# Eight quarter steps of the modulation rows m2 and m5, moved from the h2 stage into the rwkv stage

## The chip, the cores and the metric

The kernel runs on one core of a Trainium2 chip. The metric is the device time of one execution in microseconds (us). The core's engines are PE (TensorE, matmuls), DVE (VectorE), ACT (ScalarE), POOL (GpSimd) and SP (SyncE, which here mostly issues DMAs). Each engine executes its own list of instructions in order; engines wait for each other and for DMAs through semaphores.

## What is computed

Two transformer-like blocks run one after the other on 512 tokens of width 1024. The first is modulated by a conditioning vector (adaLN) and mixes an RG-LRU with dilated attention. The second makes a mixture of three branches (a multi-scale pooling, a differential attention, and a bidirectional rwkv-like recurrence) and ends in 32 experts. Each block's modulation is a long vector of silu(c) times a weight matrix:

```
mod = jnp.einsum('bd,de->be', jax.nn.silu(c), w_ada) + b_ada     # 1 row x (n*1024)
h   = rms_norm(x, g) * (1.0 + scale) + shift                     # shift, scale: rows of mod
x   = x + gate * ...                                             # gate: a row of mod
```

The second block has six such rows of 1024 numbers. Two of them, here m2 (the gate of the mixture's result) and m5 (the gate of the experts' result), are read for the first time near the end of the program: the mixture's residual and the experts' sum. The other four are needed for the norms.

## The kernel before

The program is one long function for one core. Its parts in order of time are: the first block; the h2 stage (the norm of its result x1, modulated and transposed into four pairs of tiles h2h and h2l, high and low parts of fp32); the rwkv stage; the differential attention; the merge of the branches (pm, wbr), the output projection (po) and the router; and the experts, in which the wires of the DMA queues carry 387 GB/s nearly without a break.

Nobody writes the order of instructions by hand. The code is written in one sequence, and a scheduler turns it into one list per engine: at each point it takes, of the instructions whose inputs are there, the one that was written first. So where a piece is written sets its rank, and where it lands follows from what is ready. Tiles come from pools with fixed numbers of buffers; the pool for weights has two raw buffers (512 KB each), three high parts and three low parts in this stretch, and they are handed out in the order in which the code is written. A later tile waits until the buffer it is given has been read for the last time.

**Modulation rows.** `row_steps` (L373) makes one row in four quarters of 256 columns. One quarter (L376 to L393) loads 256 numbers of bias on SP, loads two pieces of the weight matrix (512 KB each, L298), multiplies them by silu(c) in 16 matmuls (L384, m2p or m5p), copies the four partial sums out of PSUM on ACT (L386), adds them in one matmul (L388), adds the bias on DVE (L389; for m2 also a scale, L391) and stores 256 numbers to DRAM on SP (L392). The generators of all rows stand in the list `fill`, and `step(n)` (L352) runs the next n quarters of it wherever the code calls it. Of 28 quarters, 20 are run inside the dilated attention of the first block. The last eight (m2 and m5, four each) are run at two places of the h2 stage: four ahead of `norm_rows` (`step(MS[3])`, L1079) and four behind `mod_T` (`step(MX)`, L1084).

**The rwkv stage** (L1087 on) has twelve batches. `batch(n)` (L1336) writes, for batch n, `ph_a` (L1128: the products pA of receptance and key tiles, and their transposes ptb), `ph_i` (L1178: the pieces for the triangular inverse), and for the batch before it the DVE loop `ph_s` (62 operations on LT), and for batch n-2 `ph_b` (L1206: the inverse's last steps pi, px, pW, pz, and the recurrence in chunks, 16 pch matmuls and the DVE updates SI each). Written between them, but of lower rank, are projections of h2: `proj_tok` (tile pt, 256 columns; q, k and v) and `proj_feat` (tile pf, 512 columns; keys, pooling and gates). A projection needs one weight buffer, converted by ACT (wh, L305) and DVE (wl, L306), and three matmuls for each product (L311 to L313). They fill PE where a batch waits.

On PE the recurrence of one batch ends with two groups of pch matmuls, one for each chunk. The second group of a batch serves below as the mark of how far the recurrence is: in the trace that of batch 1 begins at 707.5 us, that of batch 4 at 828.4, that of batch 7 at 948.3, that of batch 8 at 979.2, and that of batch 11, the last, at 1084.8. The stretch from one such mark to the next is called a run.

Of the kernel before, what the change touches and what calls it, by code (L numbers as in the profile page):

```python
# [186 lines left out]
def build(tc, A, out, dbg=None, upto=99):  # L187
    with ExitStack() as ctx:
        _build(ctx, tc, A, out, dbg, upto)


def _build(ctx, tc, A, out, dbg, upto):
# [89 lines left out]
    def cc(name):  # L282
        g, o, w = _COFF[name]
        return csts[g][:, o:o + w]
# [67 lines left out]
    def step(n=1):  # L352

        while n and fill:
            try:
                next(fill[0])
                n -= 1
            except StopIteration:
                fill.pop(0)
# [276 lines left out]


    yb = []
    MX = 4
    MS, MA = (0, 0, 0, 4), (3, 2)  # L640
    bias1 = cc("bias1")
    def att_scores(ft, e):

# [273 lines left out]
    def cstep(n=1):  # L917
        for _ in range(n):
            next(cx, None)
# [163 lines left out]
    cstep(99)  # L1083
    step(MX)  # L1084

# [21 lines left out]
    def w1(name, shape=(4, 64), bufs=1, dt=F32):  # L1107
        p = rp if name == "AZ" else rpa if name in EARLY else rpb
        return p.tile([128] + list(shape), dt, tag=name, name=name, bufs=bufs)

    def bc(ap, sh):
        return ap.to_broadcast(sh)
# [65 lines left out]
    def ph_i(d, AMB, bi):  # L1178

        for e in range(2):  # L1180
            for i in range(2):
                r0 = 64 * e + 32 * i
                SY.dma_start(atD[bi][e, i].rearrange("q s t -> s q t"),
                             AMB[r0:r0 + 32, e, :, :, 32 * i:32 * i + 32].rearrange("p s f t -> p (s f) t"))
        LT = w1("LT", (32, 32), 2)
        for g in range(4):
            SY.dma_start(LT[32 * g:32 * g + 32].rearrange("p s t -> p (s t)"),
                         atD[bi].rearrange("e i q s t -> (e i q) (s t)"))
        return LT

    def ph_s(d, LT, bi):

        T = w1("Ti", (8, 32), 2)
        SY.dma_start(T.rearrange("p j t -> p (j t)"), A["tinit"])
        tmp = w1("Tm", (8, 32))
        for s in (range(31) if d == 0 else range(31, 0, -1)):
            js, ts_ = (slice(0, s // 4 + 1), slice(s + 1, 32)) if d == 0 else (slice(s // 4, 8), slice(0, s))
            nj, n = js.stop - js.start, ts_.stop - ts_.start
            V.tensor_tensor(tmp[:, :nj, :n], bc(LT[:, s, None, ts_], [128, nj, n]),  # L1199
                            bc(T[:, js, s:s + 1], [128, nj, n]), ALU.mult)  # L1200
            V.tensor_tensor(T[:, js, ts_], T[:, js, ts_], tmp[:, :nj, :n], ALU.add)  # L1201
        td = ttD[bi].rearrange("e i q (j g) t -> g (e i q) j t", g=4)
        for g in range(4):
            SY.dma_start(td[g], T[32 * g:32 * g + 32])
# [122 lines left out]
    def run_b():  # L1327
        n, sts = pend.pop(0)
        ph_b(*sts)
        if n == 3 and dbg is not None and "S_c" in dbg:  # L1330
            for d_ in range(2):
                for e, rows in par:
                    SY.dma_start(dbg["S_c"][128 * d_:128 * d_ + 128][rows, 256 * e:256 * e + 256],
                                 SI[d_, e][rows].rearrange("p a b -> p (a b)"))

    def batch(n):  # L1336
        d, chs = batches[n]
        AMB = w1("AMB", (2, 2, 4, 192), 3)
        sts = {c - min(chs): ph_a(d, c, c - min(chs), AMB) for c in chs}
        LT = ph_i(d, AMB, n % 4)  # L1340
        while loops:
            ph_s(*loops.pop(0))
        loops.append((d, LT, n % 4))
        pend.append((n, (d, chs, sts, AMB, n % 4)))
        if len(pend) > 2:
            run_b()
# [42 lines left out]
        GP.memset(t, 0.0)  # L1389
    for n in range(4, 12):  # L1390
        batch(n)
    ph_s(*loops.pop(0))
    while pend:
        run_b()
# [744 lines left out]
```

## Time and profile before

| | before |
|---|---|
| median of three runs | 1863.11 us (1859.43 to 1864.79) |
| the profiled execution | 1868.35 us |
| its span in the profile | 1866.5 us |
| PE busy | 1715.4 us (92% of the span) |
| DVE busy | 1068.7 us (57%) |
| ACT busy | 617.4 us (33%) |
| POOL busy | 230.4 us (12%) |

The profile is of one execution. The span runs from the first to the last instruction; the execution's own time is 1.9 us longer. An engine's busy time is the time in which it executes at least one instruction. PE has two clock levels, 1.2 and 2.4 GHz, and the profile gives the mean granted clock of a stretch as a share of the higher one: 1.00 is 2.4 GHz throughout.

### The profile page before, as it was taken

What the parts mean: (1) busy time and instruction counts of PE and PEld (TensorE: products, weight loads), DVE (VectorE), ACT (ScalarE), POOL (GpSimd) and SP (SyncE); (2) the same over time, 40 slices, a digit from 0 to 9 for tenths busy, and PEclk for the clock granted to TensorE, in tenths of its full rate; (3) what the DMA queues carried; (4) which work ended last, traced back from release to release, by engine and by line L of the source; (5) the groups of instructions that cost most, each with busy time, mean ns of one, the idle gap of its engine ahead of it and who ended that gap; (6) DMA issues with size and microseconds to landing.
All of it is one profiled execution on the core that took longest, in us unless ns stands there. A gap on an engine that the chain in (4) does not pass through costs nothing.

```text
span 1866.5 us, 31358 instructions
## 1 busy us (share of the span) xinstructions
PE 1715.4 (92%) x12309; PEld 1216.4 (65%) x12310; DVE 1068.7 (57%) x2489; ACT 617.4 (33%) x1154; POOL 230.4 (12%) x254
## 2 busy tenths in 40 slices
PE   5899998977998899999999969989799999999998
PEld 3884577964665777888888846779644544444444
DVE  3545577374578856989888538865513333432332
ACT  4324555453443232344333324542311111111010
POOL 0110003001104102212200015100100001010100
PEclk8999999987898998999999989999899999999999
DMA  8335723467847555556654367628189999999997
GB/s 295 126 110 198 237 79 124 160 213 210 232 130 183 158 171 126 157 166 157 181 142 122 102 225 240 223 67 311 46 302 387 386 386 386 387 387 387 386 386 275
DMA packets 277744, 417.34 MB, mean 224 GB/s; under 512 B 105788, under 2 KB 128856, under 8 KB 277336
## 3 DMA queue, kind: packets, MB, share of 16 engines
q1 hardware_dynamic: 248696, 384.88, 61.7%
q10 hardware_dynamic: 25568, 16.78, 2.9%
q0 software_dynamic: 3328, 13.63, 2.6%
q8 instruction: 98, 1.61, 0.4%
q14 instruction: 54, 0.44, 0.1%
HBM read 371.70 MB, written 43.53 MB: 222 GB/s over the span
## 4 chain that ended last, share of the span: by engine, by line
PE 73%; DVE 11%; DMA 7%; ACT 3%; issue 3%; SPq 2%; POOL 1%; ACTq 0%; DVEq 0%; POOLq 0%
PE ped L1983 7%; PE peg L1944 6%; PE peu L1951 6%; PE pf L311 5%; PE pf L313 4%; PE pf L312 4%; PE pcb L2015 3%; PE po L1806 2%; PE pt L311 2%; PE pt L313 2%; PE pt L312 2%; PE pg L1917 2%; PE pg L1918 2%; DVE Tm L1199 1%; DMA kb<-kbD 1%
## 5 line engine op out<-in xcount | busy, mean ns | idle before, releaser
L306 DVE TENSOR_TENSOR wl<-wr,wh 128x1024 fp32r<-128x1024 f32 x125 | 153.5, 1228 | 65.0 <-ACT wh L305 63.4
L305 ACT ACTIVATE wh<-wr 128x1024 fp32r<-128x1024 f32 x125 | 131.8, 1056 | 171.5 <-PE pf L312 91.9
L311 PE MATMUL pf<-h2h,wh 128*128 128x512 f32 x344 | 144.5, 420 | 10.7 <-ACT wh L305 4.7
L312 PE MATMUL pf<-h2l,wh 128*128 128x512 f32 x344 | 142.4, 414 | 0.0
L313 PE MATMUL pf<-h2h,wl 128*128 128x512 f32 x344 | 141.2, 410 | 0.0
L1983 PE MATMUL ped<-wd,hid 128*64 128x512 f32 (+1 forms) x528 | 127.6, 585 | 0.7 <-ACT hid L1967 0.7
L1944 PE MATMUL peg<-wg,hTg 128*64 128x512 f32 x512 | 127.0, 597 | 0.0
L1951 PE MATMUL peu<-wu,hTg 128*64 128x512 f32 x512 | 125.1, 594 | 0.0
L2016 DVE TENSOR_TENSOR acc<-acc,pcb 128x512 f32<-128x512 f32 (+1 forms) x124 | 75.9, 665 | 47.0 <-PE pcb L2015 46.8
L1989 POOL TENSOR_TENSOR yl<-ey,yh 128x512 fp32r<-128x512 f32 x30 | 38.3, 1278 | 468.1 <-ACT yh L1988 468.1
L1199 DVE TENSOR_TENSOR Tm<-LT,Ti 128x60 f32<-128x60 f32 (+24 forms) x372 | 86.3, 232 | 14.0 <-DMA LT<-atD 5.3
L1201 DVE TENSOR_TENSOR Ti<-Ti,Tm 128x60 f32<-128x60 f32 (+24 forms) x372 | 82.2, 221 | 8.6
L1951 PEld LDWEIGHTS peu<-wu,hTg 128*64 128x64 f32 x512 | 43.8, 137 | 65.2 <-issue 62.8
L311 PEld LDWEIGHTS pf<-h2h,wh 128*128 128x128 f32 x344 | 67.5, 196 | 28.8 <-ACT wh L305 5.2
L1983 PEld LDWEIGHTS ped<-wd,hid 128*64 128x64 f32 x528 | 39.4, 136 | 71.4 <-issue 67.7
L1944 PEld LDWEIGHTS peg<-wg,hTg 128*64 128x64 f32 x512 | 41.8, 137 | 60.9 <-issue 58.1
L313 PEld LDWEIGHTS pf<-h2h,wl 128*128 128x128 f32 x344 | 66.8, 194 | 21.9 <-issue 5.6
L312 PEld LDWEIGHTS pf<-h2l,wh 128*128 128x128 f32 x344 | 67.3, 196 | 17.7 <-issue 3.0
L1988 ACT ACTIVATE yh<-ey 128x512 fp32r<-128x512 f32 x30 | 18.9, 630 | 166.7 <-DVE ey L1987 94.4
L1921 ACT ACTIVATE hTg<-pg,sh,gs 128x128 f32<-128x128 f32 x64 | 28.2, 456 | 121.7 <-PE peu L1951 55.4
L1924 DVE TENSOR_SCALAR hTg<-pg,gs,sh 128x128 f32<-128x128 f32 x64 | 25.3, 409 | 75.3 <-PE peu L1951 38.4
L311 PE MATMUL pt<-wh,h1h 128*128 128x256 f32 x192 | 56.4, 296 | 6.7 <-ACT q L547 4.3
(958 smaller groups left out, 4309.4 us busy)
## 6 DMA issues: line engine op xcount, KB each, us to landing
wg<-in_w_exp_gate_dram SPq DMA_DIRECT2D x64, 1024.0 KB
wu<-in_w_exp_up_dram SPq DMA_DIRECT2D x64, 1024.0 KB
wd<-in_w_exp_down_dram SPq DMA_DIRECT2D x62, 1024.0 KB
wr<-in_w_in_dram SPq DMA_DIRECT2D x97, 512.0 KB
kb<-kbD SPq DMA_DIRECT2D x24, 384.0 KB
wr<-in_w_out_dram SPq DMA_DIRECT2D x16, 512.0 KB
LT<-atD SPq DMA_DIRECT2D x48, 128.0 KB
thD<-mth ACTq DMA_DIRECT2D x24, 256.0 KB
```

The lines of the kernel that those rows point to most:

```text
L305: SC.activation(hi, raw, AF.Copy)
L306: V.tensor_tensor(lo, raw, hi.bitcast(F32), ALU.subtract)
L311: PE.matmul(p, ah, bh, start=start, stop=False)
L312: PE.matmul(p, ah, bl, start=False, stop=False)
L313: PE.matmul(p, al, bh, start=False, stop=stop)
L1199: V.tensor_tensor(tmp[:, :nj, :n], bc(LT[:, s, None, ts_], [128, nj, n]), bc(T[:, js, s:s + 1], [128, nj, n]), ALU.mult)
L1201: V.tensor_tensor(T[:, js, ts_], T[:, js, ts_], tmp[:, :nj, :n], ALU.add)
L1944: mm = PE.matmul(pg[64 * a:64 * a + 64, :], hT[:, k, 64 * a:64 * a + 64], gp[a][k // 4][:, k % 4, :], start=(k == 0), stop=(k == 7), tile_ ...
L1951: PE.matmul(pu[64 * a:64 * a + 64, :], hT[:, k, 64 * a:64 * a + 64], up[a][k // 4][:, k % 4, :], start=(k == 0), stop=(k == 7), tile_posit ...
L1983: PE.matmul(pd[64 * a:64 * a + 64, :], hid[:, m * k + 64 * a:m * k + 64 * a + 64], dn[q][a][:, k, 0:q1 - q0], start=(k == 0), stop=(k == 3 ...
L2015: PE.matmul(p, ohT[R, 128 * i:128 * (i + 1)], yy[R, qs], start=(z == 0), stop=(z == len(parts) - 1))
L2016: V.tensor_tensor(acc[i][:, qs], acc[i][:, qs], p, ALU.add)
```

## The change

The two calls in the h2 stage run no quarters any more, and behind each of the batches 4 to 11 one quarter is written. What is computed stays the same.

```
@@ -636,8 +636,8 @@
     yb = []
-    MX = 4
-    MS, MA = (0, 0, 0, 4), (3, 2)
+    MX = 0
+    MS, MA = (0, 0, 0, 0), (3, 2)
@@ -1389,6 +1389,7 @@
     for n in range(4, 12):
         batch(n)
+        step(1)
     ph_s(*loops.pop(0))
```

What the scheduler makes of it stands at three places. Lines of the changed kernel behind L1391 have one line number more.

First, SP's list between the last stores of the first block and the first weights of the h2 projections. `m2b`, `m5b` are the bias and the result of a quarter, `m5w2r` a raw weight piece of its third quarter, `wr` a raw weight tile of the projections, `kbD` the stored keys of the recurrence, `cst` constants. Before:

```order
L379 DMA m5b<-in_bada_2r_dram 1x256
L298 DMA m5w2r<-in_w_ada_dram 128x1024
L392 DMA m2D<-m2b 1x256
L298 DMA m5w3r<-in_w_ada_dram 128x1024
L392 DMA m5D<-m5b 1x256
L379 DMA m5b<-in_bada_2r_dram 1x256
L298 DMA m5w3r<-in_w_ada_dram 128x1024
L392 DMA m5D<-m5b 1x256
L379 DMA m5b<-in_bada_2r_dram 1x256
L392 DMA m5D<-m5b 1x256
L275 DMA cst_4502<-in_cst_dram 128x514
L298 DMA wr<-in_w_in_dram 128x1024 x2
```

After:

```order
L778 DMA kbD_2113<-nb 512x1x64 x2
L275 DMA cst_4328<-in_cst_dram 128x514
L778 DMA kbD_2113<-nb 512x1x64
L778 DMA kbD_2113<-tha 512x1x64 x3
L778 DMA kbD_2113<-nb 512x1x64
L778 DMA kbD_2113<-tha 512x1x64
L298 DMA wr<-in_w_in_dram 128x1024 x5
L1132 DMA kb<-kbD_2113 128x768
L1134 DMA kr<-kkD 128x256
```

The sixteen weight pieces of the eight quarters (the last ones are shown) and all bias loads and stores are gone from here; five weight tiles of the projections follow the stores of the keys directly.

Second, PE in the rwkv stage, in the run of batch 2 (the one that begins at 707.5 us in the trace of before). `pA`, `ptb`, `pi`, `px`, `pta`, `pW` belong to a batch, `pgt` to the rwkv gate, `pt` to a projection. Before:

```order
L1260 MATMUL pi<-T_6772,AMB 32x32 x5
L879 MATMUL pgt<-gl,gw_6490 128x512
L1260 MATMUL pi<-T_6772,AMB 32x32 x11
L311 MATMUL pt<-wh,h2h_4315 128x256
L312 MATMUL pt<-wl,h2h_4315 128x256
L313 MATMUL pt<-wh,h2l_4316 128x256
L311 MATMUL pt<-wh,h2h_4326 128x256
L312 MATMUL pt<-wl,h2h_4326 128x256
L313 MATMUL pt<-wh,h2l_4327 128x256
L1162 MATMUL pA<-AR,BK 128x128 x8
L311 MATMUL pt<-wh,h2h_4337 128x256
L312 MATMUL pt<-wl,h2h_4337 128x256
```

After:

```order
L1255 MATMUL pi<-cst_75,TT_4341 32x32 x4
L384 MATMUL m2p<-m2w0r,st_945 32x256 x8
L1162 MATMUL pA<-AR,BK 128x128 x8
L1260 MATMUL pi<-T_6598,AMB 32x32 x16
L388 MATMUL m2q<-m2r,cst_75 1x256
L1171 MATMUL ptb<-cst_75,BK 128x64 x8
L1265 MATMUL pi<-TT_4341,T_6598 32x32 x16
L1273 MATMUL px<-AZ,TT_4341 64x128 x16
L1232 MATMUL pta<-cst_75,AR 64x64 x9
```

The eight quarters land in three runs, those of the batches 2, 3 and 4, and not one behind each of eight batches. The projections that stood in these runs (192 pt and 96 pf matmuls) are written later than the first quarters, take the same two raw buffers in that order, and move behind them: the runs hold batch work and quarters, and behind the last pch group there now stand 123 pf matmuls ahead of the first of the attention, where there were none.

Third, PE at the start of the differential attention. `dpl` are its scores, `dpt` and `dpo` the transposes and products of its probabilities, `pm` transposes the normalised recurrence output `gy`, which is loaded from DRAM (L1611) once the last chunk has been stored. Before:

```order
L1313 MATMUL pch<-WW,SI_4531 64x64
L1664 MATMUL dpl<-ks,qs 128x512 x2
L1617 MATMUL pm<-gy_11744,cst_75 128x512 x2
L1665 MATMUL dpl<-kl,qs 128x512
L1664 MATMUL dpl<-ks,qs 128x256
L1665 MATMUL dpl<-kl,qs 128x256
L1665 MATMUL dpl<-kl,qs 128x512
L1664 MATMUL dpl<-ks,qs 128x256
L1665 MATMUL dpl<-kl,qs 128x256
L311 MATMUL pf<-h2h_4315,wh 128x512
L312 MATMUL pf<-h2l_4316,wh 128x512
L313 MATMUL pf<-h2h_4315,wl 128x512
```

(The last three rows begin 48 pf matmuls of the gates.) After, around the first pm:

```order
L1665 MATMUL dpl<-ks,qs 128x512
L1666 MATMUL dpl<-kl,qs 128x512
L1665 MATMUL dpl<-ks,qs 128x256
L1666 MATMUL dpl<-kl,qs 128x256
L1691 MATMUL dpo<-v,aT 128x128 x4
L1691 MATMUL dpo<-vc,aT 128x128 x2
L1665 MATMUL dpl<-ks,qs 128x512
L1666 MATMUL dpl<-kl,qs 128x512
L1665 MATMUL dpl<-ks,qs 128x256
L1666 MATMUL dpl<-kl,qs 128x256
L1684 MATMUL dpt<-cst_75,P 128x128 x6
L1618 MATMUL pm<-gy_11744,cst_75 128x512
```

Before, two score matmuls stood between the last pch and the first pm. After, the 123 pf matmuls and the scores of the first three rounds, with the transposes and products of the earlier ones, stand ahead of the first pm, which come one at a time.

## Rows read from the trace of the kernel before

**Rows 1.** The page: the chain that ended last, share by engine

```profile
PE 73%; DVE 11%; DMA 7%; ACT 3%; issue 3%; SPq 2%; POOL 1%; ACTq 0%; DVEq 0%; POOLq 0%
```

**Rows 2.** Windows: from:to, length, busy PE, PEld, DVE, ACT, POOL; PE clock, DMA share, GB/s

```profile
433.00:469.00 36.00, 22.05 (x175) 8.76 (x175) 17.10 (x33) 12.80 (x27) 5.51 (x11) 0.78 0.82 258
469.00:707.50 238.50, 219.54 (x1426) 162.95 (x1426) 172.54 (x417) 94.24 (x149) 38.64 (x56) 0.92 0.62 169
707.50:828.40 120.90, 114.59 (x1277) 95.81 (x1276) 100.21 (x326) 44.90 (x91) 27.54 (x39) 0.95 0.57 145
828.40:1086.70 258.30, 247.37 (x2878) 212.24 (x2877) 201.53 (x628) 95.57 (x181) 32.94 (x52) 0.97 0.56 157
1086.70:1101.40 14.70, 1.20 (x5) 0.48 (x3) 0.85 (x2) 0.38 (x1) 1.32 (x2) 0.62 0.80 282
1200.00:1246.00 46.00, 35.61 (x216) 31.38 (x216) 31.66 (x56) 24.18 (x50) 5.59 (x5) 0.89 0.09 27
```

**Rows 3.** The chain of waits, h2 stage: start, length, what

```profile
453.53 5.10 DMA m5w2r<-in_w_ada_dram
...
463.12 4.63 DMA wr<-in_w_in_dram
467.78 1.06 ACT wh L305
```

**Rows 4.** Timeline of PE, h2 stage: start, length, what, [idle before]

```profile
444.67 0.64 PE L384 MATMUL m2p<-m2w2r,st 128*32 128x256 f32 x8 [1.33 <-DMA m2w2r<-in_w_ada_dram]
...
447.99 0.38 PE L388 MATMUL m2q<-m2r,cst 128*1 128x256 f32 x1
...
468.89 0.79 PE L311 MATMUL pf<-h2h,wh 128*128 128x512 f32 x1 [4.73 <-ACT wh L305]
...
479.31 0.40 PE L312 MATMUL pf<-h2l,wh 128*128 128x512 f32 x1
```

**Rows 5.** ACT by line from 440 to 469 us: busy, mean ns

```profile
L453 ACT ACTIVATE h2h<-h 128x512 fp32r<-128x512 f32 x8 | 4.9, 627 | 1.7 <-DMA vTD<-vTs 1.7
L449 ACT ACTIVATE h<-h2T,sh,gs 128x512 f32<-128x512 f32 x4 | 3.1, 774 | 0.3 <-PE h2T L436 0.3
```

**Rows 6.** Timeline of ACT, h2 stage: a row copy ahead of the first h

```profile
442.09 0.38 ACT L386 ACTIVATE m2r<-m2p 128x256 f32<-128x256 f32 x1 [2.86 <-PE m2p L384]
```

**Rows 7.** Windows: the run of batch 8, and a stretch at a lower clock

```profile
948.30:979.20 30.90, 30.90 (x392) 28.13 (x391) 23.63 (x84) 10.12 (x21) 1.77 (x4) 0.95 0.61 151
700.00:736.00 36.00, 32.60 (x356) 25.92 (x356) 22.12 (x75) 11.97 (x27) 5.37 (x11) 0.81 0.45 118
```

**Rows 8.** PE windows of tile pt alone, then of tile pf alone

```profile
707.50:828.40 120.90, 29.06 (x192) 0.95 0.57 145
...
948.30:979.20 30.90, 13.54 (x91) 0.95 0.61 151
...
707.50:828.40 120.90, 25.25 (x96) 0.95 0.57 145
```

**Rows 9.** PE by line in the runs of batches 2 to 4: busy, mean ns

```profile
L1480 PE MATMUL dqT<-cst,dro 128*128 128x128 f32 x16 | 2.2, 280 | 0.0
L1440 PE MATMUL pcf<-gbo,cst 128*128 128x512 f32 x4 | 2.0, 591 | 0.0
```

**Rows 10.** Timeline of DVE: the two operations of a quarter

```profile
440.34 0.41 DVE L389 TENSOR_TENSOR m2b<-m2q,m2b 1x256 f32<-1x256 f32 x1 [0.34 <-PE m2q L388]
440.79 0.28 DVE L391 TENSOR_SCALAR m2b<-m2b 1x256 f32<-1x256 f32 x1
```

**Rows 11.** Timeline of PE: the same sixteen pA matmuls at two clocks

```profile
704.56 3.09 PE L1162 MATMUL pA<-AR,BK 64*128 64x128 f32 x16
...
718.07 1.16 PE L1162 MATMUL pA<-AR,BK 64*128 64x128 f32 x16
```

**Rows 12.** Timeline of PE: between the rwkv stage and the attention

```profile
1101.39 3.78 PE L1617 MATMUL pm<-gy,cst 128*128 128x512 f32 x4 [13.50 <-POOL gy L1615]
```

**Rows 13.** The chain of waits there

```profile
1091.50 8.41 DMA gy<-yD
```

More of the change, by code (lines that the diff above doesn't have):

```diff
@@ L638, in _build @@
     yb = []
-    MX = 4
-    MS, MA = (0, 0, 0, 4), (3, 2)
+    MX = 0
+    MS, MA = (0, 0, 0, 0), (3, 2)
     bias1 = cc("bias1")
@@ L1391, in _build @@
         batch(n)
+        step(1)
     ph_s(*loops.pop(0))
```

## The prediction

> **What bounds the kernel now.** I read the page first. PE is busy for most of the span (1715.4 us, in the table) and holds 73% of the chain that ended last; DVE has 11% of it, DMA 7% [rows 1]. So a gain needs PE to stand idle less, or to run at a higher clock; taking PE work away is not on offer here, since the change only moves it. Then I read the windows by stage, and in them the PE busy time against the length of the window [rows 2]. Before the rwkv runs there is one bad stretch: from 433 to 469 us PE works for 22.05 of 36.00 us, the DMA engines are busy for 0.82 of it, and the clock is 0.78. In the first long stretch of the rwkv stage PE works 219.54 of 238.50 us, in the runs of the batches 2 to 4 114.59 of 120.90, in the rest 247.37 of 258.30: it is nearly full there, and what is moved into it competes. Then comes a hole: 1.20 of 14.70 us.
>
> Who waits in the first stretch is shown by the chain of waits: it goes through loads of the row weights (5.10 us for one piece of m5), then through a load of the projections' own weights (4.63 us), which SP could issue only behind them, and its conversion on ACT [rows 3]. On PE the first projection matmul starts at 468.89 after 4.73 us of waiting for ACT, and the last of the first chunk but one at 479.31 [rows 4]. So the eight quarters, whose rows nobody needs before the end, hold up the whole second block by some twenty us.
>
> The hole has another cause. The last chunk's result is stored, and then gy is loaded from there, which alone takes 8.41 us [rows 13]. Only two score matmuls stand on PE between the recurrence and pm, and pm then waits 13.50 us [rows 12].
>
> Behind the merges, the output projection and the experts follow in the same order in both kernels, and the change touches nothing there; a shift at the start of the attention therefore reaches the end one for one.
>
> **The change, part 1: the h2 stage.** Sixteen loads, eight bias loads and stores, the matmuls and the ACT copies go. What is late next? ACT, which converts h2. Its row copy at 442.09 ended a wait of 2.86 us for m2p [rows 6]; the first h stands right behind it and behind a copy of v. Without the rows it would begin about 2.86 us earlier, near 440.1. From there ACT has eight h2h at 0.627 us, 5.0 together, four h at 0.774, 3.1 [rows 5], and three weight tiles at 1.06 [rows 3], 3.2: 11.3, which ends at 451.4. Waits between PE's transposes and ACT of some 1 to 2 us, DVE's side of the same tiles, and the last three matmuls of the chunk (1.2 at the 0.40 of the last row [rows 4]) bring the end of the first chunk to about 455 instead of 479.7, and six matmuls of the second chunk (2.4) then already lie in it. That is 25 to 27 us at best. PE's clock was 0.78 there, and PE cannot be much faster than ACT hands it tiles; the keys of the recurrence reach DRAM no earlier than before, so the recurrence gains less than the projections do, by my reading of the order some 16. I take **-22**, with -18 and -27 as bounds.
>
> **Part 2: the runs of the batches 2 to 4.** By the order the quarters all land there. A quarter holds two raw buffers of the two that exist, so the projections that stood in these runs must wait until the last quarter's weights have been read. From the window 114.59 us of PE go away 29.06 of pt and 25.25 of pf [rows 8], with 2.2 and 2.0 of the attention's small tiles dqT and pcf [rows 9], which come behind the projections: 56 of batch work and rwkv gate stay. The quarters add, each, two groups of eight matmuls at 0.64 and one or two at 0.38 [rows 4], so about 1.9, and 15 for eight. PE would have 71 us of work in these runs. How long do they take? The trace has one run with little else in it, that of batch 8: 30.90 us, of which pt is 13.54 [rows 7, 8]. PE is full there, so it bounds a run without projections from above; I take three of them, **92.7**. From below, DVE's work in that run is 23.63 [rows 7], and a quarter adds 0.41 and 0.28 on DVE [rows 10]: 3 x 23.63 + 8 x 0.69 = 76. From above, 120.9 stays [rows 2]: the batch's own chain of products, DVE loop and chunks has then not become shorter although PE has less to do. Between these ends I take 92.7 because it comes from a run that happened. PE would be idle for about 22 us in it, that is, the space that the projections used to fill.
>
> **Part 3: the rest of the stage.** The projections come back here. All PE work from 707.5 to the attention is 114.59 + 247.37 = 362 [rows 2]; less the 56 that the three runs keep it is 306, and with an idle time of about 8, in proportion to the 11 that these windows lose now, 314. The first score starts at 707.5 - 22 + 92.7 + 314 = 1092.2 instead of 1086.7: **+5.5**. So the 22 us of the h2 stage are more than eaten: the row work (15) is paid here, on a full PE, and the rest is the new idle time of the thin runs.
>
> **Part 4: the hole.** In the new order the last chunk is followed by 123 pf matmuls and three rounds of scores before the first pm. At 0.40 each the pf alone take 49 us, and gy's load needs 8.41 [rows 13]; the 13.50 can go as a wait. But the recurrence then ends that much earlier against the end of PE's work, and the rounds of scores, which had 48 pf matmuls between them, now have none for four rounds and wait for DVE and ACT; the stretch at 1200 us, in which scores stand alone, is 77% busy at a clock of 0.89 [rows 2]. Four rounds cost about 5 us in this way. I take **-8**, with -3 and -13.5 as bounds.
>
> The sum: +5.5 - 8 = -2.5. On the profiled execution (1868.35, its span 1866.5) that gives 1865.9; that execution lies 5.2 above the median of 1863.11, so on the median the time is 1860.6. With the bounds of the h2 stage (+4, -5), of the three runs (a fifth of the way to each, 3 and 6) and of the hole (+5, -5.5), taken together by squares, its own range is 1852 to 1869.
>
> **The rivals.** *Slower: the three runs do not get shorter.* A run of a batch is a chain: pA, DVE's mask, ptb, the DVE loop, pi, px, pW, two chunks. Where PE has gaps, its clock can fall. The trace shows what that costs: the same sixteen pA take 3.09 us at one place and 1.16 at another [rows 11], and in the 36 us around it PE is busy 32.60 at a clock of 0.81 [rows 7]. If the 71 us of work take up to 1.5 times as long and every gap of the chain stays, the runs last 120.9 as before, and the time is 28.2 more than in the sum: 1860.6 + 28.2 = 1889. It decides for slower from 100.8 on, since 92.7 + 2.5 is the point of no change and 5.6 is what a measurement sees. For it: PE at 71 of 93 would be 77% busy, as at 1200 us. Against it: that stretch still has a clock of 0.89. The Trainium skill, "TensorE: Matmul & The Clock Gate", section "Part 1: The HAM clock gate (the "warmup" mystery)", says that the lower clock of 1.2 GHz is TensorE's default and that activity releases the higher one, which speaks against a change that thins PE out; the clock rows above agree in direction, and whether 77% is thin enough no row here shows.
>
> *Faster: the three runs are bounded by DVE and the hole goes wholly.* The runs take 76, which is 16.7 less, and the hole gives 13.5 rather than 8: 1860.6 - 16.7 - 5.5 = 1838. For it: in batch 8's run DVE and PE overlap so well that PE never stands; against it: the DVE loop is one chain and cannot run beside its own inputs.
>
> *The freed stretch is not gained.* If the chain of the first block (keys, values, the vT store that ACT waited 1.7 us for [rows 5]) is as late as the rows were, part 1 gives 11 rather than 22: 1860.6 + 11 = 1871.6. The order rules out that the change does nothing: the loads are gone from the stage.
>
> **How the numbers follow.** The forecast gets 0.45, the slower rival 0.22, the faster one 0.25, the third 0.08. The range has to leave out no more than 0.2: from 1838 to 1889 it keeps the forecast and the third case whole and about six tenths of each of the two outer cases. A measurement of this kernel can tell 0.3%, that is 5.6 us, from no change: faster means below 1857.5, slower above 1868.7. Faster: a third of the forecast's 0.45 (0.15) and nearly all of the faster rival (0.24), 0.39. Slower: 0.07 of the forecast, 0.22 and 0.05 of the third, 0.34. The rest, 0.27, is no change.
>
> **What would show it.** Part 1: the last matmul of chunk 0 near 457 rather than 479.7, and no loads of m2 and m5 weights in the chain of waits before 470. Part 2: batch 4's last group of chunks 93 us after batch 1's; at 121 the slower rival holds, at 76 the faster one; the PE clock of these runs tells which of gaps and clock it is. Part 3: the first score 5 us later than at 1086.7. Part 4: no wait of more than 3 us before pm, and gaps of PE between the first rounds of scores. The prediction is wrong at its root if the experts' stretch changes its length, or if PE's total busy time moves by more than 20 us, because then clock and not idle time has decided.

## The result, and the profile after

The change makes the kernel slower: 1885.38 us against 1866.27 us, medians of seven runs each on the chip; the ratio is 1.0103, 95% interval 1.0082 to 1.0124. The forecast was 1860.6 us with a range of 1838 to 1889. The time lies in the range, but on the other side of no change, where the slower rival (1889 us) had been put.

The profiled execution is one of 1885.38 us. Its page, cut to the span, the busy times, the granted clock of PE in 40 equal slices (tenths of full speed), and the chain by engine, where [rows 1] was the same of before:

```profile
span 1883.6 us, 31388 instructions
PE 1738.6 (92%) x12309; PEld 1236.0 (66%) x12310; DVE 1069.7 (57%) x2489; ACT 618.2 (33%) x1154; POOL 227.1 (12%) x254
PEclk8999999987999985699979999999899999999999
PE 72%; DVE 12%; DMA 9%; ACT 3%; issue 3%; SPq 1%; POOL 1%; DVEq 0%; ACTq 0%; POOLq 0%
```

PE executes the same 12309 matmuls as before, and is busy for 1738.6 us instead of 1715.4. That is 23.2 us more, and the span is 17.1 us longer: PE stands idle less than before and the kernel is slower all the same. The clock row has a hole in its 15th to 17th slice, from 660 to 800 us: 8, 5, 6. These are the runs of the batches 2 to 4.

The windows by stage (length, busy PE, PEld, DVE, ACT, POOL, then PE clock, DMA share, GB/s) answer to [rows 2]: the runs of the batches 2 to 4, the rest of the stage to the last chunk, the projections behind it, and the way from the first score to the first pm. The lines behind the first four cut the beginning of the thin runs into pieces of 20 us, then follow the clock more closely, and end with the first piece of 20 us that is at 1.00 again.

```profile
678.60:801.40 122.80, 104.24 (x1137) 78.50 (x1138) 78.36 (x276) 30.24 (x68) 10.21 (x24) 0.67 0.57 150
801.40:1084.30 282.90, 274.05 (x3025) 238.49 (x3027) 216.25 (x673) 105.26 (x200) 45.53 (x66) 0.94 0.55 153
1084.30:1118.40 34.10, 32.96 (x162) 24.80 (x162) 17.60 (x19) 9.75 (x14) 3.29 (x6) 1.00 0.74 264
1118.40:1129.90 11.50, 9.20 (x55) 7.41 (x54) 8.71 (x14) 7.14 (x14) 2.89 (x3) 1.00 0.14 48
...
680.00:700.00 20.00, 14.16 (x223) 11.02 (x222) 9.65 (x28) 5.90 (x13) 2.86 (x7) 0.89 0.49 127
700.00:720.00 20.00, 17.64 (x102) 12.34 (x102) 16.62 (x68) 3.92 (x9) 3.26 (x3) 0.50 1.09 246
720.00:740.00 20.00, 19.28 (x205) 13.66 (x204) 11.48 (x35) 5.25 (x12) 1.31 (x5) 0.50 0.45 120
...
692.00:695.00 3.00, 2.92 (x26) 2.93 (x28) 0.02 (x1) 0.37 (x1) 0.00 (x0) 0.52 0.39 63
696.00:698.50 2.50, 0.37 (x13) 0.23 (x7) 0.00 (x0) 0.00 (x0) 0.00 (x0) 1.00 0.55 110
...
716.40:738.20 21.80, 21.80 (x218) 15.86 (x218) 14.55 (x48) 5.74 (x14) 3.30 (x6) 0.50 0.55 148
820.00:840.00 20.00, 20.00 (x214) 17.43 (x213) 19.41 (x70) 10.05 (x19) 7.20 (x11) 1.00 0.36 101
```

The three runs take 122.8 us, as long as before (120.9 in [rows 2]), though the projections are gone from them. PE works 104.24 us there, for work that I had put at 71; the clock is 0.67 over the whole and 0.50, which is the lower level of 1.2 GHz throughout, from 700 to 740 us. From 716.4 to 738.2 PE has no gap at all (21.80 of 21.80 us) and is still at 0.50.

The timeline of PE (start, length, what, idle before) shows the h2 stage in its first two lines, what PE did before the clock fell, and the end of the stage:

```profile
445.34 0.78 PE L311 MATMUL pf<-h2h,wh 128*128 128x512 f32 x1
...
456.38 0.40 PE L311 MATMUL pf<-h2h,wh 128*128 128x512 f32 x1
...
690.67 0.69 PE L1265 MATMUL pi<-TT,T 32*32 32x32 f32 x32 [0.95 <-ACT T L1251]
692.08 3.72 PE L1273 MATMUL px<-AZ,TT 64*64 64x128 f32 x31 [0.71 <-DVE TT L1250]
...
700.07 1.33 PE L1287 MATMUL pW<-AMB,XV 128*128 128x64 f32 x5 [3.70 <-DVE XV L1276]
...
716.36 1.08 PE L384 MATMUL m2p<-m2w2r,st 128*32 128x256 f32 x8 [1.81 <-DMA m2w2r<-in_w_ada_dram]
...
1118.37 0.80 PE L1665 MATMUL dpl<-ks,qs 128*128 128x512 f32 x1
...
1129.86 1.02 PE L1618 MATMUL pm<-gy,cst 128*128 128x512 f32 x2
```

The first projection of h2 starts at 445.34 (468.89 in [rows 4]), and the first chunk is through at 456.8 (479.7 there). Gaps of 0.95, 0.71 and 3.70 us stand where projections stood before, ended by ACT and DVE of the batch itself. Behind the first two the clock is down (0.52 from 692 to 695), from 696 to 698.5 it is at 1.00, and with the third it is down again. The group of eight row matmuls at 716.36 takes 1.08 us, where the same eight take 0.64 in [rows 4]. And pm does not wait any more.

Stage by stage, from the two profiled executions (in us; "mark 1" is batch 1's last chunk group, "score" the first score, "po" the first matmul of the output projection, at 1274.3 before and 1291.4 after):

| stretch | before | after | difference |
|---|---|---|---|
| start to mark 1 | 707.6 | 678.6 | -29.0 |
| mark 1 to batch 4's last group (three runs) | 120.8 | 122.8 | +2.0 |
| from there to the first score | 258.3 | 317.0 | +58.7 |
| first score to po | 187.6 | 173.0 | -14.6 |
| po to the end | 592.2 | 592.2 | 0 |

The long third line is the work that the three runs no longer do: the change only moves it there, and what decides is that the runs did not get shorter in exchange. The -14.6 of the fourth line comes back in other kernels: in e2, e3, e5, e6, e7 and e8 below this stretch takes 172.0 to 174.3 us.

### The profile page after: what moved, and what is told of

The parts are those of the page before. It is cut to its first block, busy times and chain, and to the rows that moved or that the text cites. A ratio compares the mean times of both kernels' runs of the same rounds, so it can differ in the third digit from the quotient of the medians.

```text
span 1883.6 us, 31388 instructions
## 1 busy us (share of the span) xinstructions
PE 1738.6 (92%) x12309; PEld 1236.0 (66%) x12310; DVE 1069.7 (57%) x2489; ACT 618.2 (33%) x1154; POOL 227.1 (12%) x254
## 4 chain that ended last, share of the span: by engine, by line
PE 72%; DVE 12%; DMA 9%; ACT 3%; issue 3%; SPq 1%; POOL 1%; DVEq 0%; ACTq 0%; POOLq 0%
PE ped L1984 6%; PE peu L1952 6%; PE peg L1945 6%; PE pf L311 4%; PE pf L312 4%; PE pf L313 4%; PE pcb L2016 3%; PE pt L311 2%; PE po L1807 2%; PE pt L313 2%; PE pt L312 2%; PE pg L1918 2%; PE pA L1162 2%; DMA wr<-in_w_in_dram 2%; DVE Ti L1201 2%
## 5 line engine op out<-in xcount | busy, mean ns | idle before, releaser
L311 PE MATMUL pf<-h2h,wh 128*128 128x512 f32 x344 | 141.9, 413 | 12.9 <-ACT mth L1355 6.0
L1199 DVE TENSOR_TENSOR Tm<-LT,Ti 128x60 f32<-128x60 f32 (+24 forms) x372 | 80.7, 217 | 34.1 <-DMA LT<-atD 24.8
L1201 DVE TENSOR_TENSOR Ti<-Ti,Tm 128x60 f32<-128x60 f32 (+24 forms) x372 | 89.0, 239 | 9.0
L1922 ACT ACTIVATE hTg<-pg,sh,gs 128x128 f32<-128x128 f32 x64 | 28.2, 456 | 133.4 <-PE peu L1952 55.4
```

The source lines that it names most:

```text
L311: PE.matmul(p, ah, bh, start=start, stop=False)
```

## The experiments

Two causes were to be told apart: that PE, thinned out, ran at the lower clock (theory 1), or that the batches' own chain or the DMAs for the rows set the length of these runs and the clock is a side effect (theory 2). Later the question was where the row work could stand without doing harm. Ratios are to the kernel before, on the same chip; e4, e6 and e7 have two executions each, the others four to twelve.

| kernel | median, us | ratio, 95% interval |
|---|---|---|
| the change | 1885.38 | 1.0103 (1.0082 to 1.0124) |
| e1_late | 1886.63 | 1.0125 (1.0079 to 1.0171) |
| e2_filler | 1879.56 | 1.0077 (1.0042 to 1.0111) |
| e3_noload | 1851.86 | 0.9913 (0.9879 to 0.9948) |
| e4_drop | 1843.14 | 0.9873 (0.9825 to 0.9921) |
| e5_both | 1908.55 | 1.0220 (1.0197 to 1.0243) |
| e6_raw_only | 1908.78 | 1.0225 (1.0197 to 1.0252) |
| e7_psum_only | 1922.82 | 1.0300 (1.0257 to 1.0342) |
| e8_both_pa | 1975.24 | 1.0585 (1.0562 to 1.0608) |
| e9_all_own | 1869.79 | 1.0032 (1.0012 to 1.0052) |
| e10_half | 1867.14 | 1.0021 (1.0008 to 1.0034) |
| e11_own_hole | 1864.20 | 1.0001 (0.9985 to 1.0018) |
| e12_before_hole | 1860.01 | 0.9980 (0.9959 to 1.0000) |
| e13_attention | 1865.37 | 1.0011 (0.9989 to 1.0033) |
| e14_att_late | 1871.66 | 1.0027 (1.0007 to 1.0047) |

Single profiles scatter: e12_before_hole has the code of the kernel before up to the attention, and its mark 1 stands at 698.1 instead of 707.6. And e13 and e14 execute the same matmuls in the same order from mark 1 to the first score, but take 385.0 and 398.8 us for it (the window of e13 stands with its run below; this is that of e14):

```profile
681.30:1080.10 398.80, 382.54 (x4151) 322.75 (x4150) 301.56 (x953) 139.88 (x271) 53.40 (x91) 0.92 0.53 142
```

The clock was 0.92 instead of 0.96, and PE's work 382.54 instead of 368.32 us. So a difference of under some 14 us between two profiles proves nothing by itself.

**The quarters behind the projections (e1_late).**

```
     for n in range(4, 12):
         batch(n)
-        step(1)
```

(The calls of step(2) behind each pooling projection, which are there in both kernels and found nothing left to do, now run the eight quarters.)

> The quarters are no longer run behind the batches; they are run two at a time behind each of the four pooling projections, so the q, k and v projections are handed the raw buffers before them. Theory 1 (the projections were pushed out of the runs of batches 2 to 4, PE became thin there and lost its clock): these three runs hold projections again, their clock is above 0.9, and they take 115 to 130 us with PE nearly full; the stage start stays some 29 us earlier than in the kernel before, the row work (15 us) is paid on a full PE, the hole before pm is mostly filled: 1866 - 29 + 15 - 5 to -10, that is 1842 to 1850 us. Theory 2 (the recurrence is limited by its own chain and by what its DMAs wait for, the clock is only a side effect): the three runs still take about 122 us, and the total stays above 1870.

The runs of the batches 2 to 4 are full again, at a clock of 0.97, as theory 1 says. The total was forecast wrong by some 40 us. In the window of the last projections PE now stands idle:

```profile
687.00:806.30 119.30, 115.28 (x1260) 95.59 (x1258) 96.17 (x312) 43.52 (x87) 24.42 (x36) 0.97 0.59 159
...
1060.00:1101.70 41.70, 26.14 (x116) 13.17 (x115) 8.28 (x12) 6.14 (x11) 0.48 (x1) 0.73 0.76 257
```

```profile
1067.58 1.08 PE L384 MATMUL m5p<-m5w1r,st 128*32 128x256 f32 x8 [5.92 <-DMA m5w1r<-in_w_ada_dram]
```

The recurrence ends near 1060, 25 us earlier than before, and behind it PE goes through quarters and a few projections that wait for weights two buffers at a time (5.92 us for one piece): 26 us of work in 41.7. Then the attention takes as long as before. So theory 2's number came out, by another mechanism than theory 2's: it is the place again, here without cover.

**More work for PE in the thin runs (e2_filler).**

```
         step(1)
+        p = ps("fil", "mm")
+        for k in range(12):
+            PE.matmul(p, h2[k % 8][0][:, 0:128], h2[k % 8][0], start=(k == 0), stop=(k == 11))
```

> The changed kernel with 12 further matmuls of 128x512 behind each of its eight quarters, whose result nobody reads: 96 matmuls, about 23 us of PE work at the higher clock, all in the runs of batches 2 to 4. Theory 1 (clock): the gaps are filled, the granted clock of these runs rises from 0.67 to above 0.85, and although PE has more to do the three runs get shorter than 122.8 us, to 95 to 112, and the total falls by 10 us or more, to 1858 to 1875 us. Theory 2 (chain and DMAs): the runs stay at 122 us or grow by up to 23, total 1885 to 1908 us.

The windows of the three runs, all of PE and the filler alone (busy PE, clock, DMA share, GB/s):

```profile
679.60:795.80 116.20, 109.07 (x1229) 81.96 (x1228) 80.43 (x279) 31.76 (x70) 10.18 (x24) 0.87 0.64 168
...
679.60:795.80 116.20, 27.83 (x96) 0.87 0.64 168
```

The clock rises from 0.67 to 0.87, and the runs take 116.2 us with 96 matmuls more in them: without these PE is busy for 109.07 - 27.83 = 81.2 us, for what took 104.24 in the changed kernel. That is theory 1's direction. The size is smaller than I expected (95 to 112): 6.6 us lie within the scatter of two profiles, and the totals, 1879.56 and 1885.38, have overlapping intervals, so by length and total it is not shown. By PE's own time it is: 23 us less for the same matmuls, with the clock higher.

**Quarters that load nothing (e3_noload), and no quarters (e4_drop).**

```
-                raw = load_chunk(w, v0 * 1024 + c * 256, kt=4, name=name + "w%d" % c, nw=256, k0=4 * kh)
                 for g in range(4):
-                    PE.matmul(p[32 * g:32 * g + 32, 0:256], st[:, 4 * kh + g, :], raw[:, g, :],
+                    PE.matmul(p[32 * g:32 * g + 32, 0:256], st[:, 4 * kh + g, :], csts["0"][:, 0:256],
```

> The changed kernel with quarters that load no weights: their matmuls read a constant tile instead, all else of a quarter stays (the rows hold other numbers). No raw buffer is taken by a quarter, so the projections are not pushed back. Theory 1: projections come back into the runs from batch 3 on, the clock of 678 to 801 us is above 0.85 and the total is 1840 to 1860 us. If instead the row work itself (its place in PE's list, its waits for ACT) is what costs, the total stays above 1875 us.

```profile
688.80:788.90 100.10, 98.94 (x1225) 77.73 (x1224) 85.61 (x299) 37.70 (x81) 18.21 (x30) 0.98 0.48 123
688.80:742.00 53.20, 52.04 (x703) 37.75 (x704) 42.95 (x147) 18.69 (x44) 7.83 (x14) 0.96 0.56 143
...
688.80:1085.00 396.20, 380.50 (x4296) 318.92 (x4295) 304.93 (x968) 142.16 (x279) 55.54 (x91) 0.95 0.54 148
```

With all 128 row matmuls in place the three runs take 100.1 us at a clock of 0.98, including 25.7 us of projections, and the kernel is 0.9% faster than before. Without the projections that is about 73 us of PE work at 0.98, for what took 104 us at 0.67 in the changed kernel. So neither the place of the quarters in PE's list nor their waits for ACT cost what the change costs; their loads do, or what the loads hold. The second line says more: up to 742 us not one projection stands in e3 either, all eight quarters do, and PE is busy for 52.04 of 53.20 us at 0.96. Quarters that wait for no load fill PE as the projections did; and since these runs take 33 us each, the batches' own chain does not need the 40 that they take in the kernels before and after.

e4_drop leaves out the rows' loads, matmuls and copies altogether (only the biases are scaled and stored, so m2 and m5 are the biases alone).

> The changed kernel without the weight loads, matmuls and copies of the eight quarters: only the bias rows are scaled and stored. It shows what the freed h2 stretch alone is worth. Theory 1: batch 1's last chunk group some 29 us earlier than in the kernel before, all later stages of the same length as there, the hole before pm still about 13 us: 1832 to 1842 us. If the freed stretch is not kept (the recurrence waits elsewhere): above 1855 us.

It is 23.7 us faster than before, just outside the range for theory 1 (1832 to 1842). This is what the freed h2 stretch is worth if the rows cost nothing: an upper bound for every place of the quarters. By the medians the row work without its loads (e3 against e4) costs 8.7 us of it; the intervals of the two overlap.

**Which shared buffers push the projections out (e5_both, e6_raw_only, e7_psum_only, e8_both_pa).** The changes in `row_steps`, alone or together; the tile q is treated as p, and e8 has "pa" for "aux":

```
-            p = ps(name + "p", "mm")
+            p = ps(name + "p", "aux")
...
-                raw = load_chunk(w, ...)
                 for g in range(4):
+                    if g % 2 == 0:
+                        raw = t2(name + "w%dr" % c, w=544, tag="tp")
+                        SY.dma_start(raw[:, 0:512], w[4 * v0 * 2 + 2 * c + kh][:, 256 * g:256 * g + 512])
...
```

> The changed kernel with buffers of their own for the quarters: the weights are loaded in pieces of half the size into two small tiles that nobody else uses in this stretch, and the sums go to the PSUM tiles of the tag aux instead of mm. The same 8 MB are loaded on SP's queue, the same matmuls are made; in PE's list the projections pt now stand in every run. Theory 1 (the quarters take the raw and PSUM buffers ahead of the projections, PE becomes thin and loses its clock): clock of the runs of batches 2 to 4 above 0.9, total 1845 to 1860 us. Theory 2 (the loads themselves cost: traffic on the DMA queues and waits in SP's list): as the changed kernel, above 1875 us.

> As the kernel with both kinds of own buffers, but only the weight tiles are the quarters' own; the sums stay in the PSUM tag mm, whose two buffers the projections take too, behind the last quarter. In PE's list the projections then stand only behind the quarters, which reach into batch 6. Theory 1: still thin, clock below 0.85 in the runs of batches 2 to 4, total 1870 to 1895 us. If the raw buffers alone were the cause: below 1860 us.

> The other half: the sums go to PSUM tag aux, the weights stay in the two raw buffers that the projections use. In PE's list the quarters are spread over the batches and the first q projection stands behind the last quarter, later than in the changed kernel. Theory 1: thin over more runs, clock below 0.85 in the runs of batches 2 to 4, total 1880 us or more. If the PSUM buffers alone were the cause: below 1860 us.

> As the kernel with both kinds of own buffers, with the sums in the PSUM tag pa (of the batches' products pA) instead of aux. Theory 1: as there within 8 us, 1845 to 1865 us; a batch's pA may wait for a quarter's load once or twice, which would be seen as a wait of pA and cost a few us each. Theory 2: above 1875 us.

All four are slower than the change, and for e5 and e8 the expectation began with a wrong sentence: I had read a few projection rows ahead of the quarters as projections in every run. Counted in the trace, the first pt or pf behind the first quarter stands behind the last quarter in all four. A third kind of buffer held them back: the quarter's row and bias took two of the six small tiles (tag t1) into which the q and k projections are written. What these kernels do show is what thin runs cost. In e5 the quarters are spread as the change meant it, one in a run, from 708 to 920 us, with no projection among them (48 pt matmuls stand ahead of the first). The lines are the three runs, the stretch of the quarters, and the end of the stage:

```profile
686.00:789.00 103.00, 91.26 (x1075) 72.47 (x1076) 77.60 (x279) 27.90 (x61) 9.35 (x21) 0.76 0.54 139
...
708.00:920.50 212.50, 185.21 (x2453) 150.51 (x2449) 180.81 (x655) 64.16 (x141) 15.18 (x39) 0.78 0.49 128
...
1007.20:1144.00 136.80, 123.12 (x667) 101.91 (x667) 61.50 (x89) 37.44 (x59) 22.63 (x31) 0.93 0.64 200
```

Three runs take 103.0 us at a clock of 0.76, the recurrence is over at 1007, some 78 us earlier than before, and 136.8 us, mostly of projections, follow.

**All three kinds of buffers of their own (e9_all_own).** The kernel e5 with one more change; the line also moves behind the loads and matmuls of the quarter.

```
-            r, b = (t2(name + z, w=256, tag="t1") for z in "rb")
+            r, b = (t2(name + z, w=544, tag="tp")[:, 0:256] for z in "rb")
```

> As the kernel with own weight and PSUM buffers, and now the quarter's two small SBUF tiles (its row and its bias), which came from the six buffers of the tag t1 that the q and k projections use too, are the quarter's own as well. In PE's list projections stand in every run, and one quarter behind each of the eight batches. Same loads, same matmuls, same SP queue. Theory 1 (a quarter hands its buffers out ahead of the projections, in whichever pool they share): runs of batches 2 to 4 with projections, clock above 0.9, total 1845 to 1862 us, near the kernel whose quarters load nothing (1852). Theory 2 (the loads, their traffic and SP's queue): above 1875 us.

Now projections do stand in every run and one quarter behind each batch. The stretch from mark 1 to the first score, which in the kernel before is [rows 2]'s two windows together (379.2 us, PE 361.96):

```profile
684.40:1088.70 404.30, 385.82 (x4296) 316.84 (x4295) 309.04 (x965) 143.17 (x279) 58.25 (x91) 0.95 0.59 164
```

```profile
1103.90 3.78 PE L1620 MATMUL pm<-gy,cst 128*128 128x512 f32 x4 [14.48 <-POOL gy L1618]
```

It is 35.5 us shorter than in the changed kernel (439.8), with the same 8 MB loaded, so theory 2 falls as the main cause: PE's work went from 411.25 to 385.82 us, its idle time from 28.6 to 18.5. The total is 1869.79 and not 1845 to 1862. Against the kernel before, mark 1 is 23 us earlier, and the stretch is 25 us longer, 24 of them PE work. The recurrence is again the last thing ahead of the attention, and the hole before pm, which the change had filled, is back: 14.48 us. How much of the miss is the hole is what e11 asks.

The same stretch in the kernels that execute all the row work in it (PE busy and idle in us):

| kernel | length | PE busy | PE idle | clock |
|---|---|---|---|---|
| before (no row work here) | 379.1 | 361.9 | 17.2 | 0.96 |
| the change | 439.8 | 411.2 | 28.6 | 0.87 |
| e1_late | 415.5 | 384.4 | 31.1 | 0.95 |
| e2_filler, less the fillers' 27.8 | 424.8 | 375.9 | 21.1 | 0.96 |
| e3_noload | 396.2 | 380.5 | 15.7 | 0.95 |
| e5_both | 458.3 | 413.7 | 44.6 | 0.86 |
| e6_raw_only | 459.9 | 415.0 | 44.9 | 0.87 |
| e7_psum_only | 470.7 | 420.4 | 50.3 | 0.84 |
| e8_both_pa | 523.8 | 458.0 | 65.8 | 0.79 |
| e9_all_own | 404.3 | 385.8 | 18.5 | 0.95 |

Where the clock is 0.95 or 0.96 the row work and the rest together take 376 to 386 us of PE; where it is 0.84 to 0.87, 411 to 420, and at 0.79, 458. The number of matmuls differs by less than 1%. The gap between the two groups (25 us) is wider than the 14 us by which PE's work differed in e13 and e14.

**Half of the change (e10_half).**

```
-    MS, MA = (0, 0, 0, 0), (3, 2)
+    MS, MA = (0, 0, 0, 4), (3, 2)
```

> Half of the change: m2's four quarters stay in the h2 stage where the kernel before has them, m5's four are written behind the batches 4 to 7. In PE's list they land in the runs of batches 2 and 3, with no projections beside them, where the whole change has three such runs. Theory 1: some half of the freed stretch (13 us) is gained and two of three thin runs are paid: the first score some 20 us later than in the kernel before, total 1872 to 1885 us. Theory 2 (cost by the loads): half of the change's cost, 1874 to 1878 us; this run tells the two apart only by its clock: below 0.8 in the two runs by theory 1.

Faster than forecast, 1867.14. The clock is low, as expected, in the run of batch 2 and in the stretch behind it, up to batch 4's first group; the last quarter ends at 739:

```profile
679.30:719.00 39.70, 31.52 (x343) 22.68 (x342) 26.67 (x94) 9.70 (x22) 5.18 (x13) 0.73 0.75 191
719.00:791.00 72.00, 65.49 (x749) 55.14 (x748) 53.18 (x179) 23.11 (x46) 9.40 (x15) 0.79 0.46 128
```

```profile
453.50 0.51 PE L311 MATMUL pf<-h2h,wh 128*128 128x512 f32 x1 [3.42 <-ACT wh L305]
```

What I had wrong is the gain: mark 1 stands at 679.3, as early as with the whole change (678.6). The first projection of h2 starts at 453.50, 15.4 us earlier than before, where the whole change has 445.34; so m2's quarters do hold the projections up by 8 us, but at mark 1 nothing of that is seen beyond the scatter. For that second half the change pays with a third thin run.

**The hole before pm (e11_own_hole, e12_before_hole).** pm is queued behind the last score matmul written so far, and its first call comes one round later:

```
             pm = ps("pm")
-            PE.matmul(pm, cc("bones"), y, start=True, stop=True)
+            with tc.issue_after(lastm[0].ins):
+                PE.matmul(pm, cc("bones"), y, start=True, stop=True)
...
-    S2, OM = [2] * 16, 1
+    S2, OM = [0] + [2] * 16, 1
```

> The kernel whose quarters have all buffers of their own, with pm held back: its matmuls are queued behind the second matmul group of the third round's scores, and the side work of the recurrence's output starts one round later. In PE's list the 48 pf matmuls of the gates and some five rounds of scores then stand between the last chunk and the first pm. Theory: that kernel lost what the freed stretch gave because its first pm stands directly behind the recurrence and waits 14.5 us. The wait is gone, the scores cost some us more; the stretch from the first score to the output projection, counted with the pf ahead of it, gets 8 to 14 us shorter: total 1855 to 1862 us. If the wait only moves elsewhere (the scores, ACT): 1866 to 1872 us.

> The kernel before, with pm held back in the same way and nothing else changed. Theory: the 13.5 us wait before pm is gone, and since the quarters are not moved nothing is paid for it: total 1851 to 1859 us. If the wait only moves elsewhere: 1862 to 1868 us.

By the medians e11 is 5.6 us below e9 and equal to before; e12 gives 4.9 us. Neither reaches the range that I had for the theory. The wait at pm is gone in both, and the scores wait more, since by my reading the 48 gate matmuls that had covered them now cover the hole. The waits of PE from 680 to 1270 us (in all, times, longest), of before, of e11 and then of e12:

```profile
PE pm L1617 <- POOL gy L1615: 13.5, 1, 13.5
PE dpl L1664 <- ACT P L1667: 10.1, 6, 4.3
```

```profile
PE dpl L1670 <- ACT P L1673: 14.0, 8, 4.3
```

```profile
PE dpl L1667 <- ACT P L1670: 13.7, 8, 5.1
```

So of the 13.5 us 3.6 to 3.9 come back at the scores; where the rest of what is missing goes was not traced. e12 is the only version with the whole row work whose ratio came out below 1, by 0.2% with an interval that ends at 1.0000; that is not clear of no change.

**The row work in the attention (e13_attention, e14_att_late).** The quarters are written behind rounds of the second block's attention, and nothing of them before that; e14 has two of them behind each of the rounds 11 to 14. The cut shows the place alone; the quarters also read a copy of silu(c) there, and take their two small tiles from another ring:

```
...
+        if 5 <= n < 13:
+            step(1)
         mm = values(h, i, *cu)
```

> The quarters are taken out of the h2 stage and of the rwkv stage, and written one by one behind the rounds 5 to 12 of the second block's differential attention, beside the merges; silu(c) is copied to a tile that lives there. Theory (the change's loss is a matter of place: in the runs of batches 2 to 4 the quarters push the projections out and PE loses its clock, behind the projections nothing covers them): here the stage before is as in the kernel without quarters, PE has 27 us of gaps between the first score and the output projection to take 15 us of row work, so the total is 1846 to 1858 us. Against it: the quarters share raw and PSUM buffers with the merges and push these away from the scores; then the attention gets 15 us or more longer and the total is 1860 to 1872 us.

> The same, with two quarters behind each of the rounds 11 to 14, where in the kernel before scores stand nearly alone and PE is 77% busy. Theory (place): the quarters fill gaps that exist, 1845 to 1858 us, below the kernel with quarters at rounds 5 to 12 or equal to it. Against it: the loads of two quarters in a round are waited for as behind the last chunk (7.8 us there for one piece): above 1862 us.

Both miss the range for place and lie in the one against it. In e13 the stage before is as without quarters, and the row work is paid in the attention (windows from mark 1 to the first score and from there to po, with the wait behind):

```profile
684.60:1069.60 385.00, 368.32 (x4151) 311.36 (x4150) 302.53 (x957) 139.66 (x271) 54.24 (x93) 0.96 0.55 147
1069.60:1270.10 200.50, 175.78 (x956) 131.23 (x952) 130.25 (x205) 81.55 (x153) 40.62 (x34) 0.91 0.64 220
```

```profile
1084.68 1.22 PE L1618 MATMUL pm<-gy,cst 128*128 128x512 f32 x1 [14.01 <-POOL gy L1616]
```

The first score is 17.1 us earlier than before, and from there to po it takes 12.9 us more (200.5 against 187.6), with 15.2 us more of PE work. PE's gaps there did not take the work: it was added, not fitted in. So with the loss by the clock avoided, the move is worth about nothing in e9, e11 and e13, and e14 is slower than before (1.0007 to 1.0047).

## Why the prediction was wrong

**The bounds and part 1** were right in kind. The rows did hold up the h2 stage: the first chunk is through at 456.8 (said: 455 to 457), no weight of m2 or m5 is left in the chain there, and mark 1 comes 29.0 us earlier (said: 22, at most 27). In the other kernels with no quarter in the h2 stage mark 1 comes 19 to 29 us earlier, so 22 is inside the scatter. What I missed is that half of the quarters would have brought mark 1 as early (e10).

**Part 2 failed.** The term was 92.7 us for three runs, and they took 122.8: 30.1 us, more than the whole error of the sum. I had taken batch 8's run of 30.90 us as an upper bound for a run without projections [rows 7]. That run was at a clock of 0.95 with PE always at work, 13.54 us of it pt [rows 8]. The idle time that I allowed was right in size: 22 us forecast, 18.6 measured, 16.1 of them waits for ACT and DVE, which the projections had covered, and 2.5 for the quarters' loads. What failed is the price of the work: the matmuls that I counted as 71 us, at the lengths they have at the higher clock, took 104.2 at 0.67. The count itself was right, since e3 executes about the same work in 73 us at 0.98. The trace before held the warning in [rows 11], the same pA at 3.09 and 1.16 us, and I made it a rival (the two levels of the clock differ by a factor of two, so not all of that ratio of 2.7 is clock). I gave that rival 0.22, mostly because a stretch that is 77% busy had a clock of 0.89 [rows 2]. Here PE was 85% busy at 0.67: the busy share of a window did not tell the clock. The Trainium skill, "TensorE: Matmul & The Clock Gate", section "Part 1: The HAM clock gate (the "warmup" mystery)", has activity release the higher clock; the filler run agrees (0.67 to 0.87 with more work), while the row from 716.4 to 738.2 us, busy throughout and at 0.50, shows that a busy PE need not have it.

**The slower rival** had the mechanism and the place: runs as long as before, the work 1.5 times as long (1.47 measured). Its term was 28.2 us against 30.1. That the total, 1889 us, comes so near the 1885.4 measured is in part luck: the other parts came out 10.6 us better than forecast, and the median of the kernel before, over seven runs, is 3.2 us above the one of three runs that I started from. The rival's point of decision (100.8 us) was passed by 22. The sign that I had set for a prediction wrong at its root, PE's total busy time moving by more than 20 us, came out at 23.2.

**Why PE became thin** was only half seen. I named the two raw buffers. e6 frees these, e7 the PSUM tiles, e5 both, and in none did the projections come back; only with the small SBUF tiles freed as well (e9) did they. So the ring of small tiles alone is enough (e5 and e8 leave only that one shared with the projections); the other two were not tried alone. And being pushed back is not yet the loss: in e3 the projections stand behind the last quarter too, but the last quarter is through at 739 us, with PE full until then, while in the changed kernel it ends near 799. By e3, then, it is the waiting for loads, with the buffers held, that leaves PE thin.

**Part 3** was right: 314 us from batch 4's last group to the first score, 317.0 measured. **Part 4** was right in kind and undersized: -14.6 for -8, beyond its bound of -13.5. The wait before pm went wholly, and the 123 projections behind the last chunk left the 48 gate matmuls to cover the scores; e11 and e12, which have no such projections, gain only some 5 us. The 49 us that I put on the 123 matmuls are too much: their lengths of 0.40 us overlap, and the stretch that holds them takes 34.1 us. No term rests on it.

With the measured terms the sum closes, as it must where all terms come from the same two profiles: -2.5 forecast, -7.0 (part 1), +30.1 (part 2), +3.0 (part 3), -6.6 (part 4) give +17.0, and the spans differ by 17.1. Of these misses only that of part 2 is larger than the scatter of single profiles. That behind po nothing changes holds to 0.1 us.

**What stays open:** why the stretch from mark 1 to the first score is 5.9 us longer in e13 and 19.7 us longer in e14 than before, with no row work in it; why the same order of matmuls had a clock of 0.96 in one and 0.92 in the other; and whether a place exists where the row work costs less than the 9 to 15 us that it took in e3 and e13.

## What to carry to other kernels

Work that fills the waits of a chain is part of what makes the chain fast: price its removal with the matmul times of the lower clock, not with those of a run that still had it. When a piece is written ahead of others, list every pool that both take buffers from, weights, PSUM and small tiles: one shared ring (here that of the small tiles) is enough to push the others back behind the piece's last use, and what that costs depends on how long the piece waits for its loads. And count the row work that is moved out of an idle stretch as paid in full where it arrives, until a run shows a gap that takes it.

## What the runs showed of the hardware

With ninety-six further matmuls (27.8 us of PE time) in the three runs the granted clock rose from 0.67 to 0.87, and the rest of PE's work in them went from 104.2 to 81.2 us; the runs took 116.2 us instead of 122.8, which is within the scatter. In the changed kernel the clock fell twice: to 0.52 from 692 to 695 us, behind gaps of 0.95 and 0.71 us, and, after 2.5 us at 1.00, to 0.50 with the gap of 3.70 us that ends at 700. It came back late: PE had no gap from 716.4 to 738.2 us and was at 0.50 all the while; the window from 820 us on is at 1.00 again. And the clock is not the same for the same list of matmuls: 0.96 in e13 and 0.92 in e14 over some 390 us.
